# RMS norms that transpose the unscaled rows and scale them out of PSUM, and a reworked end of the last expert

## The chip, the cores and the metric

One core of a Trainium2 chip runs the whole program. The metric is the device time of one execution in microseconds (us); shorter is better. A profile of one execution, taken by the hardware profiler, stands beside the times.

## The reference

256 tokens of 1024 channels pass two blocks, all in float32. The first block has two layers, each with a mixer of three branches (sliding-window attention, RWKV7, retention) and a gated feed-forward part (FFN). The second block has an mLSTM and Hyena mixer and 16 experts that each choose 32 tokens, and a last norm. Where the change touches it:

```python
def _rms(x, eps=NORM_EPS):
    xf = x.astype(jnp.float32)
    return (xf * lax.rsqrt(jnp.mean(xf * xf, axis=-1, keepdims=True) + eps)).astype(x.dtype)
```

Five such norms stand ahead of projections: `_rms(x) * gain` for the mixer and the FFN of each layer of the first block, and for the second block's mixer `_rms(x) * gain + bias`, with gain and bias from a conditioning vector. A sixth norm follows the last expert: the experts' outputs, weighted by routing scores and a gate, are added to x, and `_rms(x) * g_final` is the result. (The second block's norm ahead of its router has code of its own, which the change leaves as it is.)

## The kernel before, in words

**Tokens and channels.** x lies in SBUF with tokens on partitions: two halves of 128 tokens (index i), 1024 channels each. Projections need the normed x with channels on partitions, 8 blocks of 128 channels by 256 tokens (index k). Weights come as float32 tiles of 128x1024 and are split into a rounded high part (`whi`, a cast on ACT, 1.0 us) and a rest (`wlo`, a subtraction on DVE, 1.2 us); the normed x is split too (`hTh`, `hTl`), and each product is three matmuls: high by high, high by rest, rest by high.

**A norm** (`norm_T`, L358, called at L729 and L868 in each layer and at L1315 in the second block) has these steps today. For each token half, ACT squares x in two pieces of 512 with a running sum (`row_rstd`, L327), and DVE turns the sums into 1/rms with a chain of some ten steps on single columns (`rstd_col`, L334: a bit trick and three Newton iterations). DVE multiplies x by 1/rms into `xn`, in two pieces of 512. PE transposes `xn` in 128x128 pieces into four PSUM tiles of two channel blocks each. From there ACT writes the high part with the channel's gain as a scale, and DVE the rest; with a bias DVE first writes gain and bias into a temporary, which is then split. The two `xn` tiles take two of the three buffers of `wlo`.

**PSUM** has 8 banks. Up to the experts they are four pools of two buffers each: `pj` (the projections' sums), `mx`, `rx` and `ac`. The argument `tags` of `norm_T` names the pools that the norm's four transposed tiles take: before, the first two tiles take the first tag, the other two the second. `ac` with `mx` also holds the FFN's four sums, `rx` the tiles of the RWKV part and of a few small steps. `row_bc` (L953) spreads a gate's values over the partitions with matmuls of a broadcast column against the identity (tiles `mr`, pool `mx`). The Hyena filters' spectra are made by a generator (`hyena_spectra`); its matmuls (`sp`, L1035) take their tiles with

```python
r, ps = K.R.get((P, 512)), K.ps([512], tag=("mx", "rx")[o], n="sp")
```

where o is the order of the filter, 0 or 1. Parts of the generator run in layer 1; the rest is drawn by `for _ in steps` (L1316), right behind the second block's norm.

**Order of the work.** The kernel is written in a tile framework that places the waits itself and orders each engine's instructions: program order is the priority, and later work (the casts and splits of coming weights above all) is put where an engine would else wait. Weight loads go out on SP's queue, as soon as the buffer that they fill is free.

**Experts.** In the routing stage ahead of them x is held as a high and a rest part (`Router.split`) and is put together again by `Router.merge` (L1443) in four tiles, one for each 256 channels, each with both token halves. The 16 experts' weights, 12 MB for each one, are read once through a ring of nine 2 MB buffers (two of them free early, seven after the earlier pools close). An expert (`moe`, L1580) multiplies its 32 tokens by the gate and the up weights, forms the hidden values, multiplies by the down weights (tiles `ed`), weights the result (y), and spreads it over all 256 tokens (`eo`) by a matmul with a selection matrix, and DVE adds it to x: for each half n of the channels and each token half i two adds of 256. Most experts load w_down in four pieces with rows of 16 KB. The last expert loads its w_down in four pieces by the half n of the output channels and by a pair b2 of inner blocks, with rows of 2 KB, so that the first half's work can run ahead of the second's; the last piece is split further.

**Finish** (`finish`, L1651). For each of the four channel quarters and each token half ACT squares x with a running sum and POOL multiplies x by the final gain. Then for each token half there is a chain (`rstd_col`), and each quarter is scaled, on DVE or ACT, and written out by its own DMA on SP's queue, eight of 128 KB.

## Time and profile before

| what | value |
|---|---|
| median of 3 runs | 2219.8 us (2219.72, 2219.8, 2220.71) |
| the profiled execution | 2219.28 us |
| its span in the trace | 2217.2 us |
| PE busy / PE weight loads | 85 % / 59 % of the span |
| DVE, ACT, POOL busy | 47 %, 28 %, 2 % |
| mean granted clock of TensorE | 0.929 of full speed |

The span cut in 40 slices of 55 us shows the stages. Each digit is a busy share in tenths (9 is 90 % or more), PEclk is TensorE's granted clock in tenths, GB/s is what the DMA engines moved:

```profile
PE   7999999999999999999999886666667776667675
...
DVE  5867687665677767966579840001111110111101
ACT  5344544444534454444465520000000000000001
...
PEclk9999999999999999999999988888888878988887
DMA  7332586765533258676654689999999999999997
GB/s 246 113 87 87 148 279 202 237 219 165 158 111 90 86 166 264 213 232 209 211 164 143 236 345 428 427 427 427 429 427 428 427 428 427 428 428 428 427 428 280
```

The first 23 slices are the two layers and the second block's mixer, with PE at 90 % and more. From the 24th on the experts' weights come in, and the DMA row stands at 9.

### The profile page before, as it was taken

Reading aid. Unit: us, or ns where it says so; the run is one execution under the profiler, and the core shown is the slowest. Engines: PE = TensorE matmul, PEld = TensorE weight load, DVE = VectorE, ACT = ScalarE, POOL = GpSimd, SP = SyncE. Lnnn points to the kernel's source line nnn. Section 1 sums busy time; section 2 is a strip of 40 time slices with the busy share of each in tenths; the row PEclk is TensorE's granted clock in tenths of the full one; section 3 lists DMA queues with packets and bytes.
Section 4 is the critical chain, followed back from the end, with each engine's and each line's share of the span. In section 5 each row is a group of like instructions: output and inputs, shape, how many; then the busy total and the mean of one; then the engine's idle time right before and its main releaser. Section 6 shows DMA issues by size and latency. Waiting matters only on the chain.

```text
span 2217.2 us, 34062 instructions
## 1 busy us (share of the span) xinstructions
PE 1885.0 (85%) x14084; PEld 1303.4 (59%) x14084; DVE 1042.1 (47%) x2088; ACT 630.8 (28%) x1051; POOL 33.4 (2%) x118
## 2 busy tenths in 40 slices
PE   7999999999999999999999886666667776667675
PEld 7888998998988899799988831111111111111111
DVE  5867687665677767966579840001111110111101
ACT  5344544444534454444465520000000000000001
POOL 0000000000010000000000000000000000000001
PEclk9999999999999999999999988888888878988887
DMA  7332586765533258676654689999999999999997
GB/s 246 113 87 87 148 279 202 237 219 165 158 111 90 86 166 264 213 232 209 211 164 143 236 345 428 427 427 427 429 427 428 427 428 427 428 428 428 427 428 280
DMA packets 223891, 615.53 MB, mean 278 GB/s; under 512 B 29398, under 2 KB 173303, under 8 KB 199673
## 3 DMA queue, kind: packets, MB, share of 16 engines
q1 hardware_dynamic: 222712, 611.26, 73.1%
q0 software_dynamic: 1024, 2.10, 0.3%
q8 instruction: 111, 1.82, 0.3%
q14 instruction: 44, 0.35, 0.0%
HBM read 610.17 MB, written 1.05 MB: 276 GB/s over the span
## 4 chain that ended last, share of the span: by engine, by line
PE 56%; DMA 37%; DVE 4%; ACT 1%; issue 1%; POOL 0%; SPq 0%; ACTq 0%; DVEq 0%
PE pj L150 31%; DMA ring<-in_w_down_dram 15%; DMA ring<-in_w_gate_dram 12%; DMA ring<-in_w_up_dram 10%; PE fa L150 5%; PE ed L150 3%; PE op L150 3%; PE iv L150 2%; PE wo L150 1%; DVE at L166 1%; DVE wlo L166 1%; PE tp L154 1%; PE rs L150 1%; PE eg L150 0%; PE ww L150 0%
## 5 line engine op out<-in xcount | busy, mean ns | idle before, releaser
L150 PE MATMUL pj<-hTh,whi 128*128 128x256 f32 x1800 | 517.1, 287 | 0.2 <-ACT hTh L157 0.2
L150 PE MATMUL pj<-hTl,whi 128*128 128x256 f32 x1800 | 517.0, 287 | 0.2 <-DVE hTl L175 0.2
L150 PE MATMUL pj<-hTh,wlo 128*128 128x256 f32 x1800 | 514.1, 286 | 1.3 <-DVE wlo L166 1.3
L160 ACT CAST whi<-raw 128x1024 fp32r<-128x1024 f32 x330 | 344.9, 1045 | 470.6 <-PE pj L150 324.3
L166 DVE TENSOR_TENSOR wlo<-raw,whi 128x1024 fp32r<-128x1024 f32 x330 | 401.0, 1218 | 163.3 <-ACT whi L160 161.9
L150 PEld LDWEIGHTS pj<-hTl,whi 128*128 128x128 f32 x1800 | 346.1, 192 | 6.1 <-issue 1.9
L150 PEld LDWEIGHTS pj<-hTh,whi 128*128 128x128 f32 x1800 | 346.2, 192 | 4.6 <-issue 1.1
L150 PEld LDWEIGHTS pj<-hTh,wlo 128*128 128x128 f32 x1800 | 345.4, 192 | 5.1 <-DVE wlo L166 1.8
L150 PE MATMUL ed<-ring,at 128*32 128x512 f32 x1024 | 244.6, 704 | 99.9 <-DMA ring<-in_w_down_dram 95.3
L150 PEld LDWEIGHTS ed<-ring,at 128*32 128x32 f32 x1024 | 52.1, 120 | 282.1 <-DMA ring<-in_w_down_dram 149.1
L166 DVE TENSOR_TENSOR at<-ed,at 128x512 f32<-128x512 f32 x32 | 22.1, 692 | 352.2 <-PE ed L150 352.2
L157 ACT ACTIVATE at<-eg 128x512 f32<-128x512 f32 x16 | 9.6, 597 | 529.0 <-PE eg L150 529.0
L150 PE MATMUL eu<-ring,at 128*32 128x512 f32 x512 | 89.2, 832 | 73.9 <-DMA ring<-in_w_up_dram 73.9
L175 DVE SCALAR_TENSOR_TENSOR at<-at,eu 128x512 f32<-128x512 f32 x16 | 11.0, 687 | 292.9 <-PE eu L150 292.9
L150 PE MATMUL eu<-ring,xsT 128*32 128x512 f32 x512 | 89.9, 833 | 66.2 <-DMA ring<-in_w_up_dram 66.2
L150 PE MATMUL fa<-whi,at 128*128 128x512 f32 x352 | 108.9, 390 | 0.0
L160 ACT COPY at<-et 128x512 f32<-128x512 f32 (+1 forms) x32 | 13.8, 482 | 327.9 <-PE et L154 327.9
L150 PEld LDWEIGHTS eu<-ring,at 128*32 128x32 f32 x512 | 16.3, 133 | 144.3 <-DMA ring<-in_w_up_dram 114.4
L150 PEld LDWEIGHTS eu<-ring,xsT 128*32 128x32 f32 x512 | 16.8, 133 | 132.7 <-DMA ring<-in_w_up_dram 101.2
L150 PE MATMUL eg<-ring,at 128*32 128x512 f32 x512 | 67.9, 608 | 11.6 <-DMA ring<-in_w_gate_dram 11.6
L175 DVE SCALAR_TENSOR_TENSOR at<-at,p,at 128x512 f32<-128x512 f32 x84 | 62.6, 747 | 26.6 <-DMA at<-in_w_ada_dram 25.9
L175 DVE SCALAR_TENSOR_TENSOR at<-at,eg 128x512 f32<-128x512 f32 x16 | 11.0, 687 | 134.5 <-ACT at L157 134.5
(376 smaller groups left out, 2518.9 us busy)
## 6 DMA issues: line engine op xcount, KB each, us to landing
ring<-in_w_gate_dram SPq DMA_DIRECT2D x64, 2048.0 KB, 39.1
ring<-in_w_up_dram SPq DMA_DIRECT2D x64, 2048.0 KB, 27.5
ring<-in_w_down_dram SPq DMA_DIRECT2D x60, 2048.0 KB, 38.1
raw<-in_w_in_dram SPq DMA_DIRECT2D x140, 512.0 KB, 3.6
at<-in_w_ada_dram SPq DMA_DIRECT2D x96, 256.0 KB, 4.8
raw<-in_w_ffn_gate_dram SPq DMA_DIRECT2D x44, 512.0 KB, 4.6
raw<-in_w_ffn_up_dram SPq DMA_DIRECT2D x44, 512.0 KB, 3.6
raw<-in_w_ffn_down_dram SPq DMA_DIRECT2D x44, 512.0 KB, 4.3
```

The source lines that it names most:

```text
L150: self.nc.tensor.matmul(out, lhsT, rhs, start=start, stop=stop, skip_group_check=True, **kw)
L154: self.nc.tensor.transpose(out, in_, self.ident[0:n, 0:n])
L157: self.nc.scalar.activation(out, in_, f, **kw)
L160: self.nc.scalar.copy(out, in_)
L166: self.nc.vector.tensor_tensor(out, a, b, op)
L175: self.nc.vector.scalar_tensor_tensor(out, a, s, b, op0=op0, op1=op1)
```

## The change

**Norms.** `norm_rows`, `row_rstd` and `rstd_col` go. `norm_T` transposes x as it is, unscaled, into four PSUM tiles, and all four are held at once: two from the first tag and two from the second, where a third tag holds one more tile. ACT squares x in eight pieces of 256, into an arena tile. One `tensor_reduce` sums the pieces for both token halves, and one chain of two columns (`rsqrt_cols`, which was there) makes 1/rms for both. In each Newton iteration it has one step for each column and one step for both together. Two matmuls of 1/rms, broadcast, against the identity put it in a PSUM tile with tokens along the free axis, the same on all partitions, and ACT copies that to SBUF (`rb`). DVE then multiplies each of the four PSUM tiles by `rb` into an arena tile `tm`, and from `tm` gain, bias and the split go on as before. The tags become rx, pj, mx for the first norm of each layer and, by default, for the second block's norm (before: mx, rx and mx, mx), and rx, ac, pj for the second norm of each layer (before: rx with mx in layer 0, rx alone in layer 1).

**The last expert.** Its w_down comes as two ring loads for the inner blocks 0 and 1 of both halves n (rows of 8 KB), and two loads with rows of 2 KB for blocks 2 and 3, one for each n, the last of them split. The down matmuls for blocks 0 and 1 of both n run ahead of the loop over n.

**x and finish.** `merge` writes x into four tiles by channel half n and token half i, 512 channels each, with two additions; an expert's add is one of 512 where there were two of 256. `finish` squares four pieces of 512, runs one two-column chain, and multiplies by the final gain on POOL for n = 0 only; for n = 1 one DVE instruction multiplies by 1/rms and by the gain. Each token half is written by two DMAs of 256 KB, one on ACT's queue and one on SP's.

```diff
--- before.py
+++ after.py
@@ -324,58 +324,41 @@
         return t, v
 
 
-    def row_rstd(self, x, junk):
-        ss = self.st([2], "ss", 2)
-        for k in range(2):
-            self.act(junk[:, k * 512:k * 512 + 512], x[:, k * 512:k * 512 + 512], AF.Square, accum_out=ss[:, k:k + 1])
-        return self.rstd_col(ss)
-    def rstd_col(self, ss):
-        v, r = self.st([3], "ss2", 2), self.st([1], "ssr", 2)
-        v, t, h = (v[:, k:k + 1] for k in range(3))
-        r = r[:]
-        self.tt(v, ss[:, 0:1], ss[:, 1:2], ADD)
-        self.ts(v, v, 1.0 / D, 1e-6, MUL, ADD)
-        self.ts(r.bitcast(I32), v.bitcast(I32), -0.5, float(0x5F3759DF), MUL, ADD)
-        self.ts(h, v, -0.5, None, MUL)
-        for _ in range(3):
-            self.stt(t, r, r, h, MUL, MUL)
-            self.stt(r, t, 1.5, r, ADD, MUL)
-        return r
-    def norm_rows(self, x):
-        xn = [self.whp.tile([P, 1024], F32, tag="wlo", name=self.nm("xn")) for _ in range(2)]
-        for i in range(2):
-            r = self.row_rstd(x[:, i, :], xn[i])
-            for h in range(2):
-                c = slice(h * 512, h * 512 + 512)
-                self.ts(xn[i][:, c], x[:, i, c], r, None, MUL)
-        return xn
-    def norm_T(self, x, gain, bias=None, tags=("mx", "mx")):
-        xn = self.norm_rows(x)
+    def norm_T(self, x, gain, bias=None, tags=("rx", "pj", "mx")):
         hi = self.hp.tile([P, 8, T], F32R, tag="hTh", name=self.nm("hTh"))
         lo = self.hp.tile([P, 8, T], F32R, tag="hTl", name=self.nm("hTl"))
-        for k2 in range(4):
-            ps = self.ps([2, 256], tags[k2 // 2], "tp")
+        ss, v, t, r, h = (self.st([2, 4] if n == "ss" else [2], n) for n in ("ss", "ss2", "sst", "ssr", "ssh"))
+        junk = self.A.get()
+        pss = []
+        for s in range(4):
+            pss.append(self.ps([2, 256], tags[s // 2], "tp"))
+            for i in range(2):
+                for kk in range(2):
+                    k = 2 * s + kk
+                    self.tr(pss[s][:, kk, i * 128:i * 128 + 128], x[:, i, k * 128:k * 128 + 128])
+            for i in range(2):
+                self.act(junk[:, i, :], x[:, i, s * 256:s * 256 + 256], AF.Square, accum_out=ss[:, i, s:s + 1])
+        self.A.put(junk)
+        self.nc.vector.tensor_reduce(v[:], ss[:], axis=mybir.AxisListType.X, op=ADD)
+        self.ts(v[:], v[:], 1.0 / D, 1e-6, MUL, ADD)
+        self.rsqrt_cols(r[:], v[:], t[:], h[:])
+        ps, rb = self.ps([256], tags[2], "rb"), self.st([256], "rb")
+        for i in range(2):
+            self.mm(ps[:, i * 128:i * 128 + 128], r[:, i:i + 1].to_broadcast([P, P]), self.ident, True, True)
+        self.cp(rb[:], ps[:])
+        for s in range(4):
+            tm = self.A.get()
+            self.tt(tm[:], pss[s][:], rb[:].unsqueeze(1).to_broadcast([P, 2, 256]), MUL)
             for kk in range(2):
-                k = k2 * 2 + kk
-                for i in range(2):
-                    self.tr(ps[:, kk, i * 128:i * 128 + 128], xn[i][:, k * 128:k * 128 + 128])
-            tmp = None if bias is None else self.A.get()
-            for kk in range(2):
-                k = k2 * 2 + kk
+                k = 2 * s + kk
                 if bias is None:
-                    self.act(hi[:, k, :], ps[:, kk, :], AF.Copy, scale=gain[:, k:k + 1])
-                    self.stt(lo[:, k, :], ps[:, kk, :], gain[:, k:k + 1], hi[:, k, :].bitcast(F32), MUL, SUB)
+                    self.act(hi[:, k, :], tm[:, kk, :], AF.Copy, scale=gain[:, k:k + 1])
+                    self.stt(lo[:, k, :], tm[:, kk, :], gain[:, k:k + 1], hi[:, k, :].bitcast(F32), MUL, SUB)
                 else:
-                    self.ts(tmp[:, kk, :], ps[:, kk, :], gain[:, k:k + 1], bias[:, k:k + 1], MUL, ADD)
-                    self.split(hi[:, k, :], lo[:, k, :], tmp[:, kk, :])
-            if tmp is not None:
-                self.A.put(tmp)
+                    self.ts(tm[:, kk, :], tm[:, kk, :], gain[:, k:k + 1], bias[:, k:k + 1], MUL, ADD)
+                    self.split(hi[:, k, :], lo[:, k, :], tm[:, kk, :])
+            self.A.put(tm)
         return hi, lo
 
 
@@ -726,7 +709,7 @@
     nc.sync.dma_start(pv[:], W["lpar"][l])
     wl = K.pvp.tile([P, 1024], F32, tag="wl", name=K.nm("wl"))
     w_in = W["w_in"][l].rearrange("(k p) n -> p k n", p=P)
-    H = K.norm_T(x, K.lp(pv, "n1"), tags=("mx", "rx"))
+    H = K.norm_T(x, K.lp(pv, "n1"))
     cols = lambda c0: K.cols(w_in, c0)
 
 
@@ -865,7 +848,7 @@
     tap("x_mid", fl(x))
 
 
-    H2 = K.norm_T(x, K.lp(pv, "n2"), tags=("rx", "rx" if l else "mx"))
+    H2 = K.norm_T(x, K.lp(pv, "n2"), tags=("rx", "ac", "pj"))
     low()
     wg = W["w_ffn_gate"][l].rearrange("(k p) n -> p k n", p=P)
     wu = W["w_ffn_up"][l].rearrange("(k p) n -> p k n", p=P)
@@ -1440,12 +1423,12 @@
         self.K.A.put(self.x[s])
         self.xp.append((hi, lo))
 
-    def merge(self, s):
+    def merge(self, s, x):
         hi, lo = self.xp[s]
-        t = self.K.A.get()
-        self.K.tt(t[:], hi[:].bitcast(F32), lo[:].bitcast(F32), ADD)
+        for i in range(2):
+            self.K.tt(x[i][:, s % 2 * 256:s % 2 * 256 + 256], hi[:, i].bitcast(F32), lo[:, i].bitcast(F32), ADD)
         self.K.A.put(hi, lo)
-        return t
 
     def add(self, s, x):
 
@@ -1568,7 +1551,9 @@
         for t in range(4):
             xsT[1].append(A.get((P, 2, 8, 32)))
             gather(1, one, rg, K.et, "et", (t,))
-            xs.append(route.merge(t))
+            if t % 2 == 0:
+                xs.append([A.get((P, 512)) for _ in range(2)])
+            route.merge(t, xs[-1])
         og.append(A.get((P, 2, 8, 32)))
         weights(1, one)
         A.put(*one, rg)
@@ -1624,25 +1609,28 @@
             for j in range(4):
                 K.mm(pd[n][32 * j:32 * j + 32, :], hT[:, b, 32 * j:32 * j + 32], cols(j), b == 0, b == 3)
 
         if e < 15:
             raw = [K.ring(wv[:, j].rearrange("p b n -> p (b n)")) for j in range(4)]
             for b in range(4):
                 for n in range(2):
                     down(n, b, lambda j: raw[j][:, b * 1024 + n * 512:b * 1024 + n * 512 + 512])
+        else:
+            raw = [K.ring(wv[:, 2 * h:2 * h + 2, 0:2, :].rearrange("p j b n -> p j (b n)")) for h in range(2)]
+            for b in range(2):
+                for n in range(2):
+                    down(n, b, lambda j: raw[j // 2][:, j % 2 * 2048 + b * 1024 + n * 512:][:, 0:512])
         for n in range(2):
             if e == 15:
-                for b2 in range(2):
-                    raw, v = K.ring2(wv[:, :, 2 * b2:2 * b2 + 2, n * 512:n * 512 + 512], (n, b2) == (1, 1))
-                    for b in range(2):
-                        down(n, 2 * b2 + b, lambda j: v[:, b, j, :])
+                raw, v = K.ring2(wv[:, :, 2:4, n * 512:n * 512 + 512], n == 1)
+                for b in range(2):
+                    down(n, 2 + b, lambda j: v[:, b, j, :])
             y = A.get((P, 512))
             K.tt(y[:], pd[n][:], gt2[n][:], MUL)
             for i in range(2):
                 ps = K.eo.tile([P, 512], F32, tag="eo", name=K.nm("eo"))
                 K.mm(ps[:], sc[:, i, :], y[:], True, True)
-                for s in range(2):
-                    xs = x[2 * n + s][:, i, :]
-                    K.tt(xs, xs, ps[:, s * 256:s * 256 + 256], ADD)
+                K.tt(x[n][i][:], x[n][i][:], ps[:], ADD)
             A.put(y)
         A.put(hT, sc)
     return x
@@ -1650,24 +1638,21 @@
 
 def finish(K, x, junk, gfin, out):
     nc = K.nc
-    ss = [K.st([4], f"ss{i}") for i in range(2)]
-    for s in range(4):
-        c = slice(s % 2 * 256, s % 2 * 256 + 256)
+    ss, v, t, r, h = (K.st([2, 2] if n == "ss" else [2], n) for n in ("ss", "ss2", "sst", "ssr", "ssh"))
+    for n in range(2):
         for i in range(2):
-            xs = x[s][:, i, :]
-            K.act(junk[i][:, c], xs, AF.Square, accum_out=ss[i][:, s:s + 1])
-            nc.gpsimd.tensor_tensor(xs, xs, gfin[s // 2][:, c], op=MUL)
+            K.act(junk[i][:], x[n][i][:], AF.Square, accum_out=ss[:, n, i:i + 1])
+            if n == 0:
+                nc.gpsimd.tensor_tensor(x[n][i][:], x[n][i][:], gfin[n][:], op=MUL)
+    K.tt(v[:], ss[:, 0], ss[:, 1], ADD)
+    K.ts(v[:], v[:], 1.0 / D, 1e-6, MUL, ADD)
+    K.rsqrt_cols(r[:], v[:], t[:], h[:])
     ov = out[0].rearrange("(i p) d -> p i d", p=P)
     for i in range(2):
-        K.tt(ss[i][:, 0:2], ss[i][:, 0:2], ss[i][:, 2:4], ADD)
-        r = K.rstd_col(ss[i])
-        for s in range(4):
-            xs = x[s][:, i, :]
-            if s % 2:
-                K.act(xs, xs, AF.Copy, scale=r)
-            else:
-                K.ts(xs, xs, r, None, MUL)
-            nc.sync.dma_start(ov[:, i, s * 256:s * 256 + 256], xs)
+        K.act(x[0][i][:], x[0][i][:], AF.Copy, scale=r[:, i:i + 1])
+        nc.scalar.dma_start(ov[:, i, 0:512], x[0][i][:])
+        K.stt(x[1][i][:], x[1][i][:], r[:, i:i + 1], gfin[1][:], MUL, MUL)
+        nc.sync.dma_start(ov[:, i, 512:1024], x[1][i][:])
 
 
 NA1 = 24
```

## Rows read from the trace of the kernel before

**Rows 1.** Page, part 4: chain that ended last, shares of the span by engine.

```profile
PE 56%; DMA 37%; DVE 4%; ACT 1%; issue 1%; POOL 0%; SPq 0%; ACTq 0%; DVEq 0%
```

**Rows 2.** Busy by stretch, experts: us, PE, PEld, DVE, ACT, POOL, clock, DMA, GB/s.

```profile
1286.00:1294.00 8.00, 8.00 (x53) 5.36 (x55) 4.29 (x11) 4.42 (x9) 0.00 (x0) 0.91 0.00 1
1300.00:2170.00 870.00, 607.27 (x3149) 150.86 (x3141) 90.53 (x189) 27.88 (x57) 8.48 (x32) 0.85 1.01 428
2175.00:2195.00 20.00, 12.56 (x73) 3.74 (x74) 1.54 (x3) 0.86 (x2) 0.00 (x0) 0.83 1.03 383
```

**Rows 3.** The same view, three stretches around norms.

```profile
559.00:561.00 2.00, 2.00 (x14) 2.00 (x13) 1.78 (x6) 1.13 (x4) 0.00 (x0) 0.64 0.00 0
893.00:920.00 27.00, 24.13 (x131) 16.86 (x130) 26.71 (x66) 13.59 (x26) 0.00 (x0) 1.00 0.48 149
1105.60:1117.80 12.20, 12.06 (x65) 7.94 (x65) 10.21 (x34) 7.46 (x17) 0.00 (x0) 1.00 0.74 286
```

**Rows 4.** PE group sp, 1105.6 to 1117.8: busy us, mean ns, idle before.

```profile
L150 PE MATMUL sp<-rt,rt 128*128 128x512 f32 x16 | 7.7, 593 | 0.0
```

**Rows 5.** Timeline, block 2's norm: start, us, instruction, idle before and its releaser.

```profile
1107.36 2.03 PE L150 MATMUL mr<-cst,mc 128*128 128x128 f32 x16
...
1110.66 0.16 DVE L166 TENSOR_TENSOR ss<-ss 128x1 f32<-128x1 f32 x1 [1.23 <-ACT xn L157]
...
1112.19 0.22 DVE L175 SCALAR_TENSOR_TENSOR ss<-ssr,ss 128x1 f32<-128x1 f32 x1
...
1112.64 0.49 DVE L170 TENSOR_SCALAR xn<-x,ssr 128x512 f32<-128x512 f32 x1
```

**Rows 6.** Timeline, DVE, routing's two-column chain.

```profile
1272.10 0.35 DVE L175 SCALAR_TENSOR_TENSOR rst<-rsr,rsh 128x1 f32<-128x1 f32 x2
```

**Rows 7.** Groups by form, whole span, ACT and DVE: prices.

```profile
L157 ACT ACTIVATE at<-at 128x256 f32<-128x256 f32 x16 | 6.5, 408 | 20.2 <-DVE at L166 20.2
...
L160 ACT COPY at<-et 128x256 f32<-128x256 f32 x16 | 6.0, 378 | 0.0
...
L166 DVE TENSOR_TENSOR wlo<-raw,whi 128x1024 fp32r<-128x1024 f32 x328 | 399.6, 1221 | 162.3 <-ACT whi L160 160.8
...
L166 DVE TENSOR_TENSOR at<-at,eo 128x256 f32<-128x256 f32 x128 | 48.1, 417 | 31.4 <-PE eo L150 28.0
...
L166 DVE TENSOR_TENSOR at<-ed,at 128x512 f32<-128x512 f32 x32 | 22.1, 692 | 352.2 <-PE ed L150 352.2
```

**Rows 8.** Timeline, layer 1's first norm, DVE and PE.

```profile
552.76 0.16 DVE L166 TENSOR_TENSOR ss<-ss 128x1 f32<-128x1 f32 x1
...
553.60 1.11 PE L154 MATMUL tp<-cst,xn 128*128 128x128 f32 x4 [3.28 <-DVE xn L170]
555.98 2.82 PE L154 MATMUL tp<-cst,xn 128*128 128x128 f32 x12 [1.27 <-DVE xn L170]
558.45 0.56 PE L150 MATMUL pj<-hTh,whi 128*128 128x256 f32 x1
```

**Rows 9.** Timeline, layer 0's second norm, DVE and PE.

```profile
349.82 0.41 DVE L166 TENSOR_TENSOR x<-x,pj 128x256 f32<-128x256 f32 x1
...
350.69 0.83 PE L154 MATMUL tp<-cst,xn 128*128 128x128 f32 x4 [2.08 <-DVE xn L170]
...
357.06 0.56 PE L150 MATMUL pj<-hTh,whi 128*128 128x256 f32 x1
```

**Rows 10.** Timeline and one stretch, last expert and finish, PE, DVE, SP.

```profile
2191.73 1.06 PE L150 MATMUL ed<-ring,at 128*32 128x512 f32 x8 [1.49 <-DMA ring<-in_w_down_dram]
...
2204.14 1.98 PE L150 MATMUL eo<-at,at 128*128 128x512 f32 x4 [0.78 <-DVE at L166]
...
2211.42 0.16 DVE L175 SCALAR_TENSOR_TENSOR ssr<-ss,ssr 128x1 f32<-128x1 f32 x1
...
2210.83 3.78 SPq L1670 DMA_DIRECT2D out_dram<-at  x8
...
2213.00:2214.00 1.00, 0.00 (x0) 0.00 (x0) 0.00 (x0) 0.00 (x0) 0.00 (x0) 0.50 0.80 266
```

## The prediction

> **What bounds the kernel now.** I read the chain that ended last first: PE 56 %, DMA 37 % [rows 1]. Then the busy times by stretch. From 1300 to 2170 us the 16 DMA engines are full at 428 GB/s, with PE at 607 of 870 us [rows 2]: the expert stage is a weight stream. What starts it is compute. From 1286 to 1294 us every ring buffer is full and the DMA share is 0.00 [rows 2], until the first expert's matmuls free a buffer. So each microsecond won or lost before 1286 moves the end by one, and inside the stream only the last landing and what follows it count. Before the experts PE is the engine to watch: one projection after another, with gaps at the five norms.
>
> The profiled execution took 2219.28 us (span 2217.2), 0.5 us below the median of the three runs, 2219.8. The sum is made against 2219.28, and 0.5 is added at the end.
>
> **The change part by part.** *The shared chain.* Today each token half has a chain of its own on DVE: its first add starts at 1110.66 and the row scaling at 1112.64 [rows 5], 1.98 us. The new chain has two columns; the routing stage runs it already, and there a pair of column steps takes 0.35 us [rows 6] where one takes 0.22 [rows 5], so three iterations add 3 x 0.13: 2.37 us. After it now come two PE matmuls that spread 1/rms over the partitions (four records at the 2.03/16 = 0.13 us of the same form in row_bc [rows 5], 0.5 us), an ACT copy of 256 (0.38 [rows 7]) and a DVE multiply out of PSUM (0.69 [rows 7]), with some 0.2 us of handovers. The transposes leave the exposed path, since they read x unscaled. What stays hidden: xn's four multiplies against four multiplies out of PSUM, wherever DVE has room.
>
> *Second norm of layer 0.* Today the last x add waits behind the first half's chain until 349.82 although PE had gone idle at 350.69 - 2.08 = 348.6 [rows 9]; PE's projection starts at 357.06. Afterwards: add done at 349.15, last square of 256 (0.41 [rows 7]) at 349.7, 0.5 us for half a weight cast in front of it, chain 2.37, matmuls at the low clock 0.8, copy 0.38, handovers 0.2, multiply 0.69, gain copy 0.41 as the square of 256, and two handovers of 0.05: 355.2, or -1.8 us. The transposes also warmed PE: in the same place of layer 1 twelve of them took 2.82 us and the clock rose only at 560.4 (0.64 over 559 to 561 [rows 3]), 4.4 us after PE resumed at 555.98 [rows 8]. Now the projection pays that itself; I charge +0.9, half of the 1.8 us by which the low level reaches further into it. Term -0.9, bounds -2.3 (no cast, no clock) and +0.6 (a 1.22 us weight split [rows 7] inside the chain).
>
> *First norm of layer 1.* It has the tags rx, pj, mx. Transposes 2 and 3 hold both pj buffers until they are multiplied out, and the next projection needs one: PE starts after the third multiply, not after the first gain copy. From the chain's first add to that start it is now 558.45 - 552.76 = 5.7 us [rows 8]. Afterwards 2.37 + 0.8 + 0.38 + 0.2, then three multiplies with one lo step between them, 2.3: 6.05, or +0.4. Two squares of 256 for one of 512 are +0.2, the clock +0.9 as above. Term +1.5; bounds -0.8 (a start after the first multiply, no clock) and +2.7 (one more split in the chain).
>
> *First norm of layer 0.* The same steps and tags as in layer 1's first norm, which say a loss; the place of its steps beside the first weight splits is more that of layer 0's second norm, which says a gain. Between the two I take 0, with bounds -1.5 and +1.5.
>
> *Second norm of layer 1.* DVE is busy 26.71 of 27 us from 893 to 920 [rows 3]. Ten chain steps go and the four multiplies cost 0.2 us more each: 0, bounds -1.5 and +1.5.
>
> *Norm of block 2, where the forecast is decided.* PE is busy 12.06 of 12.2 us between 1105.6 and 1117.8 [rows 3], and 7.7 of that are the spectra's sp matmuls [rows 4], which fill the wait for the norm. They take their tiles from the rx pool (L1035, second order) and come after the norm in the program. Today this norm's transposes use mx. With the default tags they take both rx buffers as soon as x is there, and keep them until the first two multiplies. So nothing may run on PE between the last transpose and those: row_bc ends at 1107.36 + 2.03 = 1109.4 [rows 5], 16 transposes at 0.13 make it 1111.4; the last square, which ACT does behind row_bc's copies, lets the chain start at 1110.66 today [rows 5], 1110.9 then; chain to 1113.3, matmuls 0.5, copy 0.38, handovers 0.2, multiply 0.69: 1115.05. Idle 3.6 us less the matmuls' 0.5, plus those matmuls as new work: +3.6. Queued behind are all sp and every projection of the block. Bounds +0.5 (sp runs elsewhere) and +5.8: after 3.28 us of waiting PE came back at half clock in layer 1 [rows 8], and 4.4 us of that cost 2.2. The Trainium skill's page "Perfetto Trace Analysis", section "Identifying Performance Opportunities", says that gaps on the engine that ought to be saturated can mean too little PSUM for the next tile; by that rule the term is +3.6, and by the present row alone, which shows no gap, it would be +0.5 and the sum below 3.1 us smaller.
>
> *Last expert.* The weights' last 8.4 MB move at 383 instead of 428 GB/s [rows 2], in rows of 2 KB; half of them now go in rows of 8 KB: -1.1 us on the last landing. But today PE works after each quarter, and now the first 32 records need 4.2 MB landed, which was at 2191.73 [rows 10], say 2191.2. From there 32 + 16 + 16 records at 1.06/8 [rows 10], y 0.69 and two eo at 1.98 [rows 10] give 2202.4; PE's down part now ends at 2204.14 - 0.78 = 2203.36 [rows 10]. At half clock for the first 4.4 us it is 2204.6. Bounds -1.0 and +1.2, term 0. The Trainium skill's page "DMA: Bandwidth & Descriptors", section "Specifications", sets the least transfer for line rate at 512 B. By that rule the longer rows bring nothing, landings stay, and term and sum would be 0.5 higher; the 383 above speaks against it.
>
> *Finish.* The last eo ends at 2204.14 + 1.98 = 2206.1 [rows 10], the x add of 512 at 2206.8 (0.69), its square at about 2207.6 (0.7 for twice the 256 of 0.41, and a handover), and the chain of 2.37 at 2210.0, where today the second half's is in its last step at 2211.42 [rows 10]; the gain multiply on POOL beside it is gone for this half of the columns. Eight issues took SP 3.78 us; now two on SP, two on ACT. The 1.05 MB move at 266 GB/s [rows 10], 3.9 us, from about the same start, so bytes bind: 0 if rows of 2 KB go no faster, -1.2 if they do. Term -0.7. The wider x adds (0.69 for two of 0.42) and merges lie beside the stream: 0.
>
> **Sum:** -0.9 + 1.5 + 0 + 0 + 3.6 + 0 - 0.7 = +3.5; 2219.28 + 3.5 + 0.5 = 2223.3 us, 0.16 % over the median.
>
> **Rivals.** *Slower:* PE's clock falls in block 2's norm. For it: the 3.28 us wait above did it in layer 1; against it: the two rsqrt matmuls and the transposes lie in between. It decides once PE idles there about as long as that. It costs 2.2 more, and a split in that chain 1.2: 2226.7.
> *Faster:* the order on PE and DVE comes out better than I laid it: sp is placed before the transposes (-3.1), the four multiplies go first in both first norms (-2.3 and -1.5), the second norm at its lower bound (-1.4), the last expert at full clock with longer rows (-1.0), outputs faster (-0.5). All of it gives 2213.5. For it: the scheduler moves later work forward, as with sp today. Against: sp yields to earlier program steps, and pj has two buffers.
> *Not what it says:* the last expert's rework does nothing since PE replaces DMA as its end. That is inside my sum.
>
> **How the numbers follow.** What a measurement of this kernel can tell from no change is about 0.2 %, 4.4 us: 2215.4 to 2224.2. My sum lies in it, near its upper edge: 0.42. The slower rival, with other excess of a microsecond or two in any norm: 0.34. The faster: 0.24. The range reaches from below the faster rival's 2213.5 to the upper bounds of block 2 and one first norm together with a split (3.5 + 2.2 + 1.2 less what can't all happen at once): 2212.5 to 2229.0. The forecast's own range is 2217 to 2227.
>
> **What would show it.** In block 2's norm: a PE gap of about 3 us ended by the multiply, with sp after it; if PE stays full there, term and forecast are too high. In layer 1's first norm: the projection's start ended by a multiply out of PSUM, 5.7 to 6.5 us after the chain began. In layer 0's second norm: a start near 355. First expert's matmuls late by some 4 us. In the last expert: w_down landing a microsecond sooner and eo and down back to back. If the stream starts earlier than now, the forecast is wrong.

## The result, and the profile after

The changed kernel takes 2236.53 us, the median of four runs (2233.53 to 2237.89), against 2219.76 us for the kernel before (2219.18 to 2220.71, four runs): 1.0074 times as long, 95 % interval 1.0061 to 1.0087. The forecast was 2223.3 us in a range that ended at 2229.0. The sign of the sum was right, +3.5; the size, +16.8, is almost five times that.

The profiled execution took 2233.53 us (span 2231.7); it is the shortest of the four, 3.0 us under their median. First the chain that ended last in it, shares by engine, which answers to [rows 1]:

```profile
PE 55%; DMA 37%; DVE 4%; ACT 2%; issue 1%; POOL 0%; SPq 0%; DVEq 0%; ACTq 0%
```

The shares are almost the same (PE 55 and not 56 %); what grew has to be looked for by place. Next the waits of PE that belong to the norms: total us, number of waits, longest. First the kernel before:

```profile
PE tp L154 <- DVE xn L170: 21.1, 6, 9.1
```

and the kernel after:

```profile
PE rb L150 <- DVE ssr L175: 12.8, 4, 4.0
PE pj L150 <- DVE at L166: 8.3, 2, 4.1
PE tp L154 <- DMA cst<-in_cst_dram: 6.3, 1, 6.3
...
PE mc L150 <- DVE at L166: 1.7, 2, 1.2
...
PE sp L150 <- DVE at L166: 1.2, 1, 1.2
```

In the kernel before, PE waited 21.1 us in the norms, all of it in front of transposes, 9.1 of it at the start of the kernel. Now the transposes wait for nothing but the start of the kernel (6.3 us), and the waits stand elsewhere: four times for the chain (in front of `rb`, the matmuls that spread 1/rms), and for a multiply (DVE, L166) in front of two projections (`pj`), of the conditioning step's `mc` and of the spectra's `sp`. With the start that is 30.3 us.

Where the time went is told best by stretches that begin and end at the same matmuls in every kernel (differences of their start times in the PE timeline of each profiled execution, us; a matmul goes by the tile that it writes). The other columns are experiments, told below:

| stretch | before | after | pj_free | sp_free | free_two | free_all | free_warm | end_only | end_warm |
|---|---|---|---|---|---|---|---|---|---|
| start to first sc (layer 0's first norm) | 73.36 | 77.99 | 76.43 | 77.40 | 76.42 | 75.89 | 73.53 | 73.04 | 71.78 |
| layer 0: last out projection to first FFN down (second norm) | 33.60 | 34.60 | 33.82 | 34.73 | 34.63 | 32.97 | 31.99 | 33.60 | 33.00 |
| last FFN down to first sc (layer 1's first norm) | 66.51 | 70.58 | 67.96 | 70.63 | 67.86 | 67.89 | 65.90 | 66.47 | 65.16 |
| layer 1: second norm, as in layer 0 | 38.68 | 38.08 | 40.95 | 41.21 | 40.68 | 40.40 | 37.54 | 38.68 | 38.87 |
| lb to first iy (block 2's norm) | 61.39 | 68.25 | 68.26 | 61.67 | 61.68 | 61.70 | 61.70 | 61.40 | 61.19 |
| iy to sT (mixer and routing) | 116.50 | 114.09 | 114.07 | 114.11 | 115.62 | 115.59 | 114.09 | 115.63 | 115.59 |
| sT to the last eo (experts) | 920.60 | 922.28 | 920.49 | 920.41 | 920.21 | 919.57 | 920.52 | 919.41 | 919.30 |
| last eo to the end (finish) | 13.06 | 11.84 | 11.84 | 11.93 | 11.94 | 11.87 | 11.94 | 11.87 | 11.86 |
| median of the runs | 2220.6 | 2236.5 | 2229.9 | 2227.4 | 2223.6 | 2222.6 | 2217.5 | 2216.4 | 2214.1 |

(What is not in the table, the two layers' middles and FFNs, is 893.5 us before and 894.0 after. The kernel before was timed beside each group of experiments again, medians 2220.7, 2220.6 and 2220.3; the table has the one of 31 runs, 2218.54 to 2225.74. Each column is one execution: that of the kernel after lies 3.0 us under its median, that of free_warm 4.3 under.) Block 2's norm lost 6.9 us, the first norms 4.6 and 4.1, layer 0's second norm 1.0; finish gained 1.2.

The places themselves. Layer 0's first norm in the PE timeline of the kernel after (start, us, instruction, idle before and its releaser):

```profile
13.53 1.02 PE L150 MATMUL rb<-cst,ssr 128*128 128x128 f32 x4 [3.62 <-DVE ssr L175]
18.69 0.55 PE L150 MATMUL pj<-hTh,whi 128*128 128x256 f32 x1 [4.14 <-DVE at L166]
...
562.86 0.81 PE L150 MATMUL rb<-cst,ssr 128*128 128x128 f32 x4 [3.98 <-DVE ssr L175]
567.81 0.55 PE L150 MATMUL pj<-hTh,whi 128*128 128x256 f32 x1 [4.14 <-DVE at L166]
```

and the same norm on DVE:

```profile
14.99 1.29 DVE L166 TENSOR_TENSOR at<-tp,rb 128x512 f32<-128x512 f32 x2 [1.51 <-ACT rb L160]
16.26 1.68 DVE L175 SCALAR_TENSOR_TENSOR hTl<-at,pv,hTh 128x256 fp32r<-128x256 f32 x4
17.86 1.28 DVE L166 TENSOR_TENSOR at<-tp,rb 128x512 f32<-128x512 f32 x2
```

The third multiply, the first of the second pair, starts at 17.86 and takes 0.64; the projection starts at 18.69, behind it. The second pair of lines on PE is layer 1's first norm ([rows 8] before): the gap in front of the projection is the same, 4.14, that in front of rb 0.36 longer.

Block 2's norm ([rows 4, 5] before) on PE:

```profile
1118.81 1.91 PE L154 MATMUL tp<-cst,x 128*128 128x128 f32 x16
1123.13 1.19 PE L150 MATMUL rb<-cst,ssr 128*128 128x128 f32 x4 [2.40 <-DVE ssr L175]
1125.51 1.22 PE L150 MATMUL sp<-rt,rt 128*128 128x512 f32 x1 [1.19 <-DVE at L166]
```

and its busy times by stretch (us, then PE, PEld, DVE, ACT, POOL, granted clock, DMA share, GB/s):

```profile
1121.00:1125.00 4.00, 1.19 (x4) 0.93 (x4) 2.01 (x12) 0.37 (x1) 0.00 (x0) 0.76 1.05 400
1125.00:1130.00 5.00, 4.49 (x6) 1.91 (x7) 3.94 (x10) 1.73 (x5) 0.00 (x0) 0.51 0.46 197
```

All 16 sp records now stand behind the first multiply, and the first of them run at half clock (0.51), where the kernel before had 1.00 over the whole norm [rows 3].

### The profile page after: what moved, and what is told of

Same layout as the page of the kernel before. It is cut to its first block, busy times and chain, and to the rows that moved or that the text cites. A ratio compares the mean times of both kernels' runs of the same rounds, so it can differ in the third digit from the quotient of the medians.

```text
span 2231.7 us, 34017 instructions
## 1 busy us (share of the span) xinstructions
PE 1882.2 (84%) x14104; PEld 1308.1 (59%) x14104; DVE 1036.4 (46%) x1982; ACT 635.2 (28%) x1086; POOL 30.5 (1%) x112
## 4 chain that ended last, share of the span: by engine, by line
PE 55%; DMA 37%; DVE 4%; ACT 2%; issue 1%; POOL 0%; SPq 0%; DVEq 0%; ACTq 0%
PE pj L150 30%; DMA ring<-in_w_down_dram 16%; DMA ring<-in_w_gate_dram 12%; DMA ring<-in_w_up_dram 8%; PE fa L150 5%; PE ed L150 3%; PE op L150 3%; PE iv L150 2%; PE wo L150 1%; DVE at L166 1%; DVE wlo L166 1%; PE eo L150 1%; PE eg L150 1%; PE rs L150 1%; DMA at<-in_w_ada_dram 0%
## 5 line engine op out<-in xcount | busy, mean ns | idle before, releaser
L166 DVE TENSOR_TENSOR wlo<-raw,whi 128x1024 fp32r<-128x1024 f32 x330 | 401.4, 1219 | 189.0 <-ACT whi L160 187.9
L166 DVE TENSOR_TENSOR at<-ed,at 128x512 f32<-128x512 f32 x32 | 22.1, 692 | 355.6 <-PE ed L150 355.6
L150 PE MATMUL eu<-ring,xsT 128*32 128x512 f32 x512 | 84.4, 783 | 61.9 <-DMA ring<-in_w_up_dram 61.9
L150 PE MATMUL eg<-ring,xsT 128*32 128x512 f32 x512 | 64.4, 634 | 15.6 <-DMA ring<-in_w_gate_dram 15.6
```

What stands on the lines that cost most here:

```text
L150: self.nc.tensor.matmul(out, lhsT, rhs, start=start, stop=stop, skip_group_check=True, **kw)
L166: self.nc.vector.tensor_tensor(out, a, b, op)
```

## The experiments

The eleven kernels were timed in three groups: norms_only, end_only, pj_free and sp_free; finish_only, free_two, free_all and free_warm; best, end_warm and best_tail. Each kernel was timed in up to five rounds beside the kernel before. `norms_only` and `end_only` split the change in two.

**norms_only.** The kernel before, with the new `norm_T` and the tags of the kernel after; last expert, merge and finish as before.

```diff
-    def norm_rows(self, x):
...
+    def norm_T(...)              # the new one
...
-    H = K.norm_T(x, K.lp(pv, "n1"), tags=("mx", "rx"))
+    H = K.norm_T(x, K.lp(pv, "n1"))
...
-    H2 = K.norm_T(x, K.lp(pv, "n2"), tags=("rx", "rx" if l else "mx"))
+    H2 = K.norm_T(x, K.lp(pv, "n2"), tags=("rx", "ac", "pj"))
```

> The kernel before with the new norm_T and its tags, and nothing else of the change; the end of the last expert, merge and finish stay. Theory A (the norms carry the whole loss, the end gives back a little): in the traces of before and after the distance between the same matmuls of the two kernels grows to 16.4 us behind block 2's norm and is 14.0 us at the routing stage, and the end (last expert +1.5 for PE, weights' landings about -1.1, finish -1.1) is near -0.7; so this kernel takes 14 to 17 us more than before, about 2234 to 2237. Theory B (the end rework carries a good part of the loss): 5 to 10 us more than before. In layer 0's first norm the first pj matmul starts at 18.7 us as in the kernel after.

Measured: 2238.0 us (2233.59 to 2241.71), ratio 1.0076 (1.0063 to 1.0089), 17 us over the 2220.7 of its group. The first pj starts at 19.30 us. Theory A holds, with a time 1 us over its range: the norms carry the whole loss.

**end_only.** The kernel after, with the norms of before:

```diff
+    def row_rstd(self, x, junk):
...
+    def norm_rows(self, x):
...
+    def norm_T(...)              # the old one
...
-    H = K.norm_T(x, K.lp(pv, "n1"))
+    H = K.norm_T(x, K.lp(pv, "n1"), tags=("mx", "rx"))
...
-    H2 = K.norm_T(x, K.lp(pv, "n2"), tags=("rx", "ac", "pj"))
+    H2 = K.norm_T(x, K.lp(pv, "n2"), tags=("rx", "rx" if l else "mx"))
```

> The kernel after with the norms of before (norm_rows, row_rstd, rstd_col and their tags), so that only merge, the last expert's loads and finish are new. Theory A: -0.3 to -1.2 us against before, about 2219.0: w_down lands sooner by about 1.1, PE's down matmuls end with about +0.4 against before, finish is 1.1 shorter. Theory B (the end carries a good part of the loss): 5 us or more slower than before.

Measured: 2216.4 us (2213.89 to 2219.39), ratio 0.9978 (0.9970 to 0.9987): 4.4 us faster, where A had said at most 1.2, so both theories missed. By the table 1.2 of it is finish and 1.2 the last expert; where the remaining 2 come from isn't shown (iy to sT is 0.9 shorter in this execution, with nothing changed there). The last expert in the PE timeline of end_only:

```profile
2189.42 4.49 PE L150 MATMUL ed<-ring,at 128*32 128x512 f32 x32 [1.48 <-DMA ring<-in_w_down_dram]
2194.81 1.06 PE L150 MATMUL ed<-ring,at 128*32 128x512 f32 x8 [0.91 <-DMA ring<-in_w_down_dram]
```

and in that of the kernel after:

```profile
2205.96 8.31 PE L150 MATMUL ed<-ring,at 128*32 128x512 f32 x40 [3.07 <-DMA ring<-in_w_down_dram]
```

The same 40 records take 4.49 + 1.06 = 5.55 us in end_only and 8.31 in the kernel after: there they began behind 3.07 us of waiting, at half clock, and took back the gain. So the end of the change is worth more than the profile of the kernel after shows.

**finish_only.** The loads of the last expert taken back from end_only too:

```diff
-        else:
-            raw = [K.ring(wv[:, 2 * h:2 * h + 2, 0:2, :].rearrange("p j b n -> p j (b n)")) for h in range(2)]
...
             if e == 15:
-                raw, v = K.ring2(wv[:, :, 2:4, n * 512:n * 512 + 512], n == 1)
+                for b2 in range(2):
+                    raw, v = K.ring2(wv[:, :, 2 * b2:2 * b2 + 2, n * 512:n * 512 + 512], (n, b2) == (1, 1))
...
```

> The kernel before with the new merge, the wider x adds and the new finish, but the last expert's w_down loads and its order of before. Theory A (the finish alone gives 1.2 us, the loads of the last expert another 1.2): from the last eo matmul to the end 11.9 us in place of 13.1, the routing stage to the last eo as before (920.6 us), time 1 to 2 us under the kernel before and 1 to 3 us over end_only. Theory B (the loads bring nothing, all of end_only's gain is in finish and the x tiles): as end_only, about 4 us under the kernel before.

Measured: 2217.8 us (2214.87 to 2221.47), ratio 0.9984 (0.9975 to 0.9993), 1.4 over end_only, which the spreads don't separate. By the traces, from the routing to the last eo it is 921.03, against 919.41 with the new loads: the loads are worth 1.6 us there, finish (11.74 in place of 13.06) 1.3. Theory A for the two stretches.

**pj_free.** The kernel after, one line:

```diff
-    H = K.norm_T(x, K.lp(pv, "n1"))
+    H = K.norm_T(x, K.lp(pv, "n1"), tags=("rx", "ac", "mx"))
```

> The kernel after; the first norm of both layers takes its tiles from rx, ac and mx, in place of rx, pj and mx, so that no transposed tile holds a pj buffer. Theory A (PE waits there for the third multiply, because the transposes hold both pj buffers): the first pj matmul of layer 0 starts at about 16.3 instead of 18.69 us, behind the first hTh, and that of layer 1 about 2.5 us sooner too; 5 us less than the kernel after (4 to 6), which leaves 9 to 11 us over before. Theory B (DVE is what binds there, with the multiplies out of PSUM and the lo steps in its order): PE starts sooner, then stalls for hTl, and the time falls by under 2 us. Theory C (the wait for the chain and the low clock behind it are all of the loss): no change within 1 us.

Measured: 2229.9 us (2228.17 to 2232.34), 6.6 under the kernel after. Layer 1's first norm on PE:

```profile
560.83 0.71 PE L150 MATMUL rb<-cst,ssr 128*128 128x128 f32 x4 [3.99 <-DVE ssr L175]
563.27 0.80 PE L150 MATMUL pj<-hTh,whi 128*128 128x256 f32 x2 [1.73 <-ACT hTh L157]
```

The wait in front of the projection is 1.73 in place of 4.14 and ends with hTh, and PE then does not stall for hTl. Layer 0's projection starts at 16.88. The two stretches are 1.6 and 2.6 us shorter: theory A; the other 2.4 us of the medians are not in them, and where they come from isn't shown. The wait for the chain, 3.99, is as it was.

**sp_free.** The kernel after, one line in block 2's mixer:

```diff
-    H = K.norm_T(x, sv, mc[:, 0:8])
+    H = K.norm_T(x, sv, mc[:, 0:8], tags=("ac", "mx", "pj"))
```

> The kernel after; block 2's norm takes its tiles from ac, mx and pj in place of rx, pj and mx, so that the spectra's sp matmuls find their rx buffers free. Theory A (the transposed tiles in rx keep sp from filling PE's wait for the chain, and the clock falls in that wait): three sp matmuls run before the rb matmuls, PE's idle time of 2.4 us before rb goes to under 0.5, the granted clock stays at 1.0 over the norm, and the time is 5 us less than that of the kernel after (4 to 6.5; DVE's eight lo steps end last then and may take back 1). Theory B (sp would wait for something else, or only move): within 1 us of the kernel after.

Measured: 2227.4 us (2226.43 to 2229.87), 9.1 under the kernel after. PE in that norm:

```profile
1125.29 2.74 PE L150 MATMUL sp<-rt,rt 128*128 128x512 f32 x6
1127.87 0.61 PE L150 MATMUL rb<-cst,ssr 128*128 128x128 f32 x4
1128.32 4.46 PE L150 MATMUL sp<-rt,rt 128*128 128x512 f32 x10
1132.21 0.68 PE L150 MATMUL pj<-hTh,whi 128*128 128x256 f32 x1
```

No gap is left, and the clock stays up (the same view by stretch as above):

```profile
1119.00:1125.00 6.00, 6.00 (x52) 5.81 (x51) 3.65 (x4) 5.56 (x18) 0.52 (x1) 1.00 0.88 330
1125.00:1130.00 5.00, 5.00 (x19) 2.56 (x18) 3.18 (x15) 1.85 (x5) 0.00 (x0) 1.00 0.99 356
```

The stretch is 61.67 us, 6.6 shorter and within 0.3 of before: the two rx buffers, with the clock that fell behind the wait for them, were the whole of this norm's loss. The other 2.5 us of the medians lie outside it.

**free_two** has the edits of pj_free and sp_free together.

> The kernel after with both edits of the tags: rx, ac, mx in the first norm of both layers and ac, mx, pj in block 2's norm. Theory A (two separate waits, for a pj buffer and for an rx buffer): the gains add up; pj_free was 6.6 us under the kernel after by its median and sp_free 9.1, so 2221 to 2226 us, no more than 3 us over the kernel before. Theory B (behind the buffers DVE binds in these norms, so that the second gain is lost): over 2228.

Measured: 2223.6 us (2220.27 to 2226.26), ratio 1.0012 (1.0004 to 1.0021). The gains add up, stretch by stretch (1.6, 2.7 and 6.6 us); theory A.

**free_all** also frees rx in layer 0's second norm:

```diff
-    H2 = K.norm_T(x, K.lp(pv, "n2"), tags=("rx", "ac", "pj"))
+    H2 = K.norm_T(x, K.lp(pv, "n2"), tags=("rx" if l else "mx", "ac", "pj"))
```

> As free_two, and layer 0's second norm takes mx, ac, pj in place of rx, ac, pj, so that the conditioning step's matmuls (mc) find an rx buffer and run in PE's wait for the chain, ahead of the rb matmuls. Theory A (in the kernel after mc stands between rb and the projection, 1.9 us at the low clock): the first pj of that norm starts about 1.2 us sooner in relation to the rb matmuls' start, time 1 to 2 us under free_two. Theory B (the projection starts when hTh is there, whatever stands before): within 0.5 us.

Measured: 2222.6 us (2218.32 to 2225.8), ratio 1.0006 (0.9997 to 1.0015). That norm on PE in the kernel after:

```profile
354.26 1.91 PE L154 MATMUL tp<-cst,x 128*128 128x128 f32 x16
359.01 1.22 PE L150 MATMUL rb<-cst,ssr 128*128 128x128 f32 x4 [2.84 <-DVE ssr L175]
361.43 1.87 PE L150 MATMUL mc<-cst,at 128*128 128x1 f32 x8 [1.19 <-DVE at L166]
363.15 0.77 PE L150 MATMUL pj<-hTh,whi 128*128 128x256 f32 x2
```

and in free_all:

```profile
354.86 0.95 PE L150 MATMUL mc<-cst,at 128*128 128x1 f32 x8
358.15 0.71 PE L150 MATMUL rb<-cst,ssr 128*128 128x128 f32 x4 [2.34 <-DVE ssr L175]
360.59 0.80 PE L150 MATMUL pj<-hTh,whi 128*128 128x256 f32 x2 [1.73 <-ACT hTh L157]
```

From rb to pj it is 2.44 us and not 4.14, and the stretch is 1.66 shorter. Theory A for the stretch; the medians differ by 1.0, which their spreads don't separate.

**free_warm** keeps PE at work in the waits that are left, with products of the identity that nothing reads:

```diff
+        ps, rb = self.ps([512], tags[2], "rb"), self.st([256], "rb")
+        for _ in range(warm[0]):
+            self.mm(ps[:, 256:384], self.ident, self.ident, True, True)
         self.nc.vector.tensor_reduce(v[:], ss[:], axis=mybir.AxisListType.X, op=ADD)
...
         self.cp(rb[:], ps[:, 0:256])
+        for _ in range(warm[1]):
+            self.mm(ps[:, 384:512], self.ident, self.ident, True, True)
...
```

> As free_all, and PE multiplies the identity by itself into the unused half of rb's PSUM tile while it waits: in layer 0's first norm 7 times ahead of the rb matmuls and 3 times behind them, in its second norm 8 and 5, in layer 1's first norm 15 and 5 (0.25 us each at full clock); nothing of the computation changes. Theory A (a good part of what is left is TensorE's clock, which stands at half behind each idle stretch): the granted clock of the first 6 us of each of these three projections goes from about 0.5 to 0.9 or more, records of 128x256 start 0.12 us apart there and not 0.21; 4 to 8 us under free_all. Theory B (the clock costs nothing on the path, DVE's multiplies and lo steps would hold PE anyway): within 1.5 us of free_all, with PE waiting for hTl at full clock.

Measured: 2217.5 us (2213.15 to 2220.27), ratio 0.9984 (0.9974 to 0.9993), 5.1 under free_all. The first 6 us of the three projections, by stretch, in free_all:

```profile
17.07:23.07 6.00, 6.00 (x34) 5.77 (x35) 5.94 (x14) 5.12 (x10) 0.00 (x0) 0.68 0.70 225
360.59:366.59 6.00, 6.00 (x31) 5.98 (x32) 5.19 (x12) 3.31 (x8) 0.00 (x0) 0.58 0.46 143
563.00:569.00 6.00, 6.00 (x35) 5.98 (x36) 4.53 (x10) 3.76 (x8) 0.00 (x0) 0.67 0.01 3
```

and in free_warm:

```profile
16.03:22.03 6.00, 5.86 (x45) 5.67 (x46) 5.95 (x13) 5.04 (x10) 0.00 (x0) 1.00 0.83 266
357.31:363.31 6.00, 6.00 (x40) 5.86 (x40) 5.33 (x12) 3.83 (x8) 0.00 (x0) 0.75 0.40 129
558.42:564.42 6.00, 5.98 (x49) 5.78 (x48) 5.55 (x12) 3.79 (x8) 0.00 (x0) 1.00 0.00 0
```

The third number from the end of a line is the granted clock: 0.58 to 0.68 without the products, 0.75 to 1.00 with them. PE is busy for 5.86 to 6.00 of the 6 us in both, but gets 40 to 49 records done in place of 31 to 35. The three stretches are 2.4, 1.0 and 2.0 us shorter; in layer 0's first norm about 0.5 of it is a chain on DVE that ended sooner in this execution (13.53 in place of 14.06), which the products on PE don't explain. Theory A: the rest is the price of the clock behind an idle PE, and a busy share of 100 % hides it.

**best** adds `(0, 6)` such products in layer 1's second norm, behind the rb matmuls. PE waits there in front of `hy`, matmuls of the Hyena filters' generator.

```diff
-    ..., warm=((0, 0) if l else (8, 5)))
+    ..., warm=((0, 6) if l else (8, 5)))
```

> As free_warm, and six more multiplications of the identity behind the rb matmuls of layer 1's second norm, where PE waits 1.2 to 1.7 us for the filters' next step. Theory A (in five of the six kernels with the new norms whose profiles stand here the granted clock falls to half behind that wait for some 6 us, which makes that stretch 2.5 to 3 us longer): the stretch from the last out projection to the first FFN down matmul of layer 1 is 37.5 to 38.1 us long; time 1 to 3 us under free_warm's 2217.5. Theory B (the clock falls there for another reason): within 1 us of free_warm.

Measured: 2217.2 us (2215.41 to 2219.94), no different from free_warm. PE there:

```profile
908.32 1.13 PE L150 MATMUL hy<-at,hid 64*128 64x512 f32 x2 [0.60 <-DVE rt L175]
...
911.15 2.93 PE L150 MATMUL rb<-cst 128*128 128x128 f32 x12
```

The products (the last line) came behind the wait, which stands in front of hy; they filled nothing and cost their own 2.93 us at half clock. The stretch was 39.88 us, so the expectation missed; whether products ahead of hy would help was not tried.

**end_warm.** The same idea in the norms of before, on top of end_only: products ahead of the first transposes and between those of the two token halves. The edit also takes the first two PSUM tiles ahead of the chain and names the order of their transposes, which in the traces hardly changes.

```diff
+        pss = [self.ps([2, 256], tags[0], "tp") for _ in range(2)]
+        for _ in range(warm[0]):
+            self.mm(pss[0][:, 0, 0:128], self.ident, self.ident, True, True)
         xn = self.norm_rows(x)
...
+            for _ in range(0 if i else warm[1]):
+                self.mm(pss[1][:, 1, 128:256], self.ident, self.ident, True, True)
...
```

> As end_only (the norms of before), and PE multiplies the identity by itself in the waits of the first norms and of layer 0's second norm, ahead of the first transposes (6, 8 and 12 times) and between those of the two token halves (4, 11 and 4 times); nothing of the computation changes. Theory A (the clock's price is that of any norm that leaves PE idle, and the old norms pay a smaller one since their transposes come late and warm PE): 2 to 4 us under end_only's 2216.4. Theory B (the old norms pay no clock): within 1 us of end_only. Against the run called best this tells what the new norms give or cost once buffers and clock are out of it: by the traces of free_warm and end_only the new norms then differ by +0.5 us in layer 0's first norm, -0.6 in layer 1's and -1.6 in layer 0's second.

Measured: 2214.1 us (2210.92 to 2215.65), ratio 0.9969 (0.9958 to 0.9981): the fastest of all by its median, 2.3 under end_only (timed in another group; against the kernel before beside each it is 1.9) and 22 under the kernel after. The three stretches gain 1.3, 0.6 and 1.3, less than the 2.4, 1.0 and 2.0 of the new norms: both pay the clock, the new ones more.

**best_tail** adds 14 products ahead of the last expert's down matmuls to best.

```diff
+            dm = K.eg.tile([P, 512], F32, tag="eg", name=K.nm("dm"))
+            for _ in range(14):
+                K.mm(dm[:, 0:128], hT[:, 0, :], K.ident, True, True)
             for b in range(2):
```

> As best, and 14 multiplications of a hidden tile by the identity ahead of the last expert's down matmuls, while PE waits for w_down, into a PSUM tile that nothing reads. Theory A (in the kernel after the last 40 down records of the first stretch take 8.3 us, half of it at the low clock, on the path that ends last): from the routing stage to the last eo 1.5 to 3 us less than in best, time 1.5 to 3 us less. Theory B (the weights' last landing sets the end): within 0.7 us of best.

Measured: 2220.4 us (2216.67 to 2222.42), 3.1 over best. From the routing to the last eo it is 919.41 and not 920.48, 1.1 less: the 40 records take 5.55 us in place of 7.04, and then PE waits 0.86 us for the last landing. A is right about the clock, and its number was too large. But layer 1's second norm took 43.44 us in this execution, 3.6 more than in best, and iy to sT 1.5 more, with the same order of matmuls in both. In both places the granted clock stood lower than in best: 0.50 over 8 us in the norm, where best has 0.62 over 4 us and then 1.00; the last section shows the second place. The median is higher too; why the clock falls there in the one execution and not in the other stays open.

## Why the prediction was wrong

**Block 2's norm** was named as the place where the forecast is decided, with the right cause: the transposes hold both rx buffers, sp has to wait. The term was +3.6, the stretch lost 6.9, and sp_free gave back 6.6. The idle time came out as laid out, 2.40 + 1.19 = 3.6 us. What failed is the size: the fall of the clock was kept apart as the slower rival, at 2.2 more, though the gap and the clock behind it are one event. At the low clock the rb matmuls took 1.19 us where 0.5 was laid out, and the 16 sp records 8.8 from the first start to the projection, where sp_free ran them in 6.5. The Trainium skill, in its page "Perfetto Trace Analysis", section "Identifying Performance Opportunities", says that the same gap repeating on the engine that should be saturated can mean too little SBUF or PSUM for the next tile. This gap stood once and did not repeat, but its cause was the one that the page names: two buffers, 6.6 us.

**Layer 1's first norm**, +1.5 with +2.7 as its bound, lost 4.1; **layer 0's**, 0 within 1.5, lost 4.6. The mechanism was right here too (both pj buffers held until the third multiply). The step that failed is "three multiplies with one lo step between them, 2.3": on DVE four lo steps (the instructions that write hTl) stand between the second and the third multiply, and from the end of the copy of rb (14.96) to the projection it is 3.7 us in layer 0. In layer 1 the chain of the kernel after begins here:

```profile
560.42 0.16 DVE L343 TENSOR_REDUCE ss<-ss 128x2 f32<-128x8 f32 x1 [0.26 <-ACT at L157]
```

From there to the projection at 567.81 it is 7.4 us, where 6.05 was laid out and 6.5 was the upper end of the sign to look for: 1.4 more, all of it in that step. The chain also began 0.9 us later behind the last FFN down matmul than in the kernel before (0.2 was laid out), and from the projection to the first sc it took 1.5 more (0.9 was charged for the clock). pj_free gave back 1.6 and 2.6. In layer 0 two weight splits of 1.2 us also fell into the chain, which ran from 8.71 to 13.48.

**The clock** was charged at 0.9 in two norms and not at all in layer 0's first. free_warm priced it at about 1.9 (2.4 less what the chain gave there), 1.0 and 2.0. The half by which I cut the charge had no row behind it.

**Layer 0's second norm** was to gain 0.9 and lost 1.0. The add of x was not freed: a weight split stood in front of it on DVE (355.12 is where the split of 353.98 ends), and another between it and the chain. And the mc matmuls, 1.87 us at the low clock, stood between rb and the projection, since they wait for an rx buffer (in free_all, with rx free, they run ahead of rb); they were in no step of mine, though the same buffers were the point of the argument in block 2.

**Layer 1's second norm** was forecast unchanged: -0.6 in this profile, but +1.7 to +2.5 in five others with the same norms, where the clock fell.

**The last expert**, 0 from -1.0 to +1.2, is worth -1.6 to -1.2 where PE comes at full clock (single traces, as said above), and was lost to the low clock in the profile of the kernel after. **Finish**, -0.7, is -1.2, the bound that was written for it if rows of 2 KB go faster, and they did: in the kernel after the outputs reached 385 GB/s, where the last line of [rows 10] has 266.

```profile
2229.00:2230.00 1.00, 0.00 (x0) 0.00 (x0) 0.00 (x0) 0.00 (x0) 0.00 (x0) 0.50 1.00 385
```

The Trainium skill, in its page "DMA: Bandwidth & Descriptors", section "Specifications", sets the least transfer for line rate at 512 B. By that rule the longer rows of the last expert's weights would have given nothing. Measured over 10 us each, the first line from the kernel before (the beginning of the last line of [rows 2]) and the second from the place in the kernel after that answers to it, the engines moved 387 GB/s and then 418. (An expert's weights are 24 MB and not 12: the gate weights of all 16 experts come in 64 loads of 2 MB, 8 MB for each expert, and the up and the down weights are as large.)

```profile
2175.00:2185.00 10.00, 5.20 (x34) 1.32 (x35) 0.69 (x1) 0.00 (x0) 0.00 (x0) 0.84 1.02 387
2189.04:2199.04 10.00, 5.53 (x35) 1.34 (x36) 0.69 (x1) 0.00 (x0) 0.00 (x0) 0.83 1.00 418
```

**The range** left out what "can't all happen at once". In four of the five norms it did, and the parts have one cause: the change puts all transposes ahead of one chain, so PE idles through it, its clock falls, and the tiles that wait for the multiply hold what PE could have done meanwhile. The three numbers that the range's upper end was built from, 3.5 + 2.2 + 1.2, make 2226.7 on 2219.8; how 2229.0 follows from them isn't said. The upper bounds of all terms together (0.6 + 2.7 + 1.5 + 1.5 + 5.8 + 1.2 + 0) are 13.3 us; with 0.5 they would have reached 2233.1, still 3.4 under what was measured. So it was not only the range that was too narrow: in four norms the loss lies beyond the bound of its own term.

**And what is left of the idea.** With buffers and clock out of it (free_warm) layer 0's two norms, layer 1's first and block 2's differ from those of end_only by +0.5, -1.6, -0.6 and +0.3 us; with the clock mended in the old ones too (end_warm) by +1.8, -1.0, +0.7 and +0.5, 2.0 on the whole, and free_warm's median is 3.4 us higher than end_warm's (they were timed in different groups). So one chain in front of all of a norm's work gained nothing in these runs over two chains, of which the first runs while the last rows are still being added.

## What to carry to other kernels

A tile that is produced early to shorten a chain holds its PSUM buffer until the end of that chain: list what else takes its buffers from that pool, and choose the pools that the next work doesn't need; two changed tuples of tags were worth 13 us here by the medians, 10.9 in the three norms that they concern. Price an idle PE by its wait and by the slow records behind it together, and read the clock in the row: a PE that is 100 % busy at half clock looks full. Losses that have one cause belong together in the upper end of a range.

## What the runs showed of the hardware

In layer 1's second norm PE runs the same matmuls in the same order in several of these kernels, and waits in front of hy. Behind 1.18 us of idle time (after) the granted clock stayed at 1.00; behind 1.49 (norms_only) it fell:

```profile
921.43:923.43 2.00, 1.60 (x6) 0.63 (x4) 2.00 (x4) 1.07 (x3) 0.00 (x0) 0.74 0.00 0
923.43:925.43 2.00, 2.00 (x11) 2.00 (x11) 2.00 (x6) 1.30 (x4) 0.00 (x0) 0.50 0.75 235
```

The stretch was 38.08 us in the one and 41.09 in the other. But in best the clock fell behind 0.60 us of idle time, and in free_warm it did not behind 0.49 (nor behind 0.64 in front of mc, right after): the length of the wait alone doesn't order these cases.

Between iy and sT, where no experiment changes the matmuls, every trace has a wait of 1.03 or 1.04 us for DVE in front of a transpose (yT). Here are the 8 us from that transpose on, in best and in best_tail:

```profile
1251.94:1259.94 8.00, 7.19 (x54) 6.51 (x55) 4.88 (x8) 2.30 (x4) 0.00 (x0) 1.00 1.00 426
1255.65:1263.65 8.00, 7.18 (x42) 6.51 (x43) 3.41 (x6) 1.28 (x3) 0.00 (x0) 0.79 1.01 428
```

PE is busy for the same time in both and gets 54 records done in the one and 42 in the other. The clock stayed at 1.00 there in five of the thirteen traces (after, best, free_warm, pj_free, sp_free), and iy to sT took 114.1 us in all five; it fell in the other eight, which took 115.6 or more. That is the 1.5 us by which most columns of the table differ in a stretch whose matmuls no edit touches. So a difference of 1.5 us (here) or 3 us (layer 1's second norm) between two single executions can be the clock alone. Each kernel has one trace, so whether executions of one kernel differ in this way isn't shown; the runs of the kernel before lie up to 7.2 us apart.
